# Down projection of a conditioned decoder block: 24 products of f-tile groups, or seven half-size products formed from sums

## The chip, the cores and the metric

The kernel runs on one core of a Trainium2 chip. The metric is device time in microseconds (us). The engines are PE (TensorE: matrix products; PEld is its weight load), DVE (VectorE), ACT (ScalarE), POOL (GpSimd) and SP (SyncE), the last of which issues most DMA transfers; ACT issues some. SBUF is the memory on the core with 128 partitions, PSUM holds the products' sums in banks of 128 x 512 fp32, DRAM lies outside the core.

## The reference

One block with S = 1024 tokens, D = 1024 channels and FF = 2816 hidden channels, all fp32. The part that the change touches is its last two lines.

```
h = rms_norm(x, norm_mix_g) * (1 + sc1) + sh1
proj = h @ w_in + b_in
y_conv  = silu(layer_norm(conv31(a))) @ w_conv_pw + b_conv_pw
y_mlstm = sigmoid(o_pre) * mlstm(q, k, v, gates)
x = x + g1 * ((g_conv * y_conv + g_mlstm * y_mlstm) @ w_out)
...
h = rms_norm(x, norm_ffn_g) * (1 + sc2) + sh2
gt, up = split(h @ w_ffn_up)
x = x + g2 * ((silu(gt) * up) @ w_ffn_down)
return rms_norm(x, final_norm_g)
```

## The kernel before

An fp32 product is made of three fp32r products: each operand is split into hi (a copy on ACT) and lo (raw minus hi, on DVE), and hi x hi, lo x hi and hi x lo are summed in PSUM. An instruction multiplies a stationary 128 x 128 block with a moving block of 128 x 512.

The program runs in stages: modulation and first norm, the input projection beside convolution and mLSTM, the output projection, the up projection with the SwiGLU, and the down projection with the final norm. The framework's scheduler decides the order of instructions on each engine, from the order in which the code gives them out and from its own timeline.

**Up projection.** FF is cut into 22 f-tiles of 128 channels; the loop at L1232 takes f = 2 to 21, and f-tiles 0 and 1 run before it in halves of the tokens (L1221 to L1230). For each, `up_run` (L1118) makes seven products of half size with the moving tiles Bh/Bl, Th/Tl and Dh/Dl, and sums them to the gate half cg and the up half cu, each [128, 512] for two token halves. The last lines, L1148 to L1155, apply Silu, multiply, and store cg to act_d in DRAM as [f within tile, f-tile, token], two transfers of 256 KB for an f-tile, in pieces of 1 KB, through ACT's queue (SP's for the last f-tile). In the last pass four rows of w_down are loaded and split for the first group.

**Down projection.** The 22 f-tiles are taken in `groups` of 4, 4, 6 and 8 (L1158). Within a group the loop runs over 8 token tiles t of 128: `act_split` (L1175) loads this group's activations of the token tile, transposed as they were stored, and splits them (stationary operand, tiles wraw, whi, wlo); then for both halves of the 1024 output columns come 3 products for each f-tile of the group (L1299 to L1301). The weights are `down_raw` (L1160: a 128 x 1024 row block of w_down, multiplied by the row g2) and `down_split` (L1165: hi and lo in tiles fa or, for the third group, fb). One row block of the next group is prepared for each token tile (PACE). A group's sums are added to the residual x1 on DVE (L1303); in the last group `finish` (L1262) adds, squares with a sum, multiplies by the final norm's gain, scales by the reciprocal root (a power on POOL, L104) and stores.

**Memory.** The tiles xa and xb (pool `big`) and wraw, whi, wlo (pool `wp`) live through both stages. Pool `fp`, opened after the up projection (L1246), takes the space that the up projection's own pools (`up`, and `tp` with Th and Tl) held, so what it holds waits for their last readers. All DMA issues of SP and ACT share a rotation of eight semaphores.

Of the kernel before, what the change touches and what calls it, by code (L numbers as in the profile page):

```python
# [33 lines left out]
PACE = 1  # L34
# [9 lines left out]
MC0 = 6152  # L44
MM0 = MC0 + 1024


@with_exitstack
def hybrid_block(ctx: ExitStack, tc: tile.TileContext, x, c, w_ada, b_ada, norm_mix_g, w_in, b_in,
# [903 lines left out]
    act_d = dram.tile([128, FT, S], F32, name="act_d")  # L953
# [164 lines left out]
    def up_run(f, w, half=None):  # L1118
# [29 lines left out]
        for i in range(2):  # L1148
            nc.scalar.activation(cg[i], cg[i], AF.Silu)
            nc.vector.tensor_mul(cg[i], cg[i], cu[i])  # L1150
            dst = act_d[:, f, :].rearrange("p (a b c) -> p b a c", a=2, b=2)
            if half is None:
                (nc.sync if f == FT - 1 else nc.scalar).dma_start(dst[:, i], cg[i].rearrange("p (a c) -> p a c", a=2))
            else:
                nc.scalar.dma_start(dst[:, i, half, :], cg[i])  # L1155
        yield

    groups = [4, 4, 6, 8]  # L1158

    def down_raw(f, raw, row):  # L1160
        nc.sync.dma_start(raw, wdn[f * 128:(f + 1) * 128, :])
        nc.vector.tensor_mul(raw, raw, row)
        return raw

    def down_split(gidx, i, raw):  # L1165
        if gidx == 2:
            hi, lo = (fp.tile([128, D], F32R, name=f"fb{j}", tag=f"fb{j}", bufs=6) for j in range(2))
        else:
            tag = "xa" if gidx == 0 or (gidx == 3 and i < 4) else "xb"
            hi, lo = (big.tile([128, D], F32R, name=f"fa{j}", tag=tag) for j in range(2))  # L1170
# [4 lines left out]
    def act_split(f0, nf, t):  # L1175
        raw, hi, lo = (wp.tile([128, KT, 128], dt, name=n, tag=n)[:, 0:nf, :]
                       for n, dt in (("wraw", F32), ("whi", F32R), ("wlo", F32R)))
        nc.sync.dma_start(raw, act_d[:, f0:f0 + nf, t * 128:(t + 1) * 128])
        nc.scalar.activation(hi, raw, AF.Copy)  # L1179
        nc.vector.tensor_sub(lo, raw, hi.bitcast(F32))  # L1180
        return hi, lo
# [50 lines left out]
    for f in range(2, FT):  # L1232
        w_f, w = w, up_split(up_sums(f + 1)) if f + 1 < FT else None
        if f == FT - 1:
            row = kx("g2row")
            mod_row(1, row)
            raws = [down_raw(i, (k4 if i < 2 else kx)("draw"), row) for i in range(4)]
        steps = up_run(f, w_f)
        next(steps)
        next(steps)  # L1240
        if f == FT - 1:
            wd = [down_split(0, i, raw) for i, raw in enumerate(raws)]
# [43 lines left out]
    for gidx, nf in enumerate(groups):  # L1286
# [4 lines left out]
        for t in range(8):  # L1291
# [3 lines left out]
            if gidx < 3:  # L1295
                p = ps_mm()
# [40 lines left out]
```

## Time and profile before

| | us |
|---|---|
| median of 3 runs | 1733.2 (1731.33 to 1735.08) |
| the profiled execution | 1735.88 |
| its span | 1734.1 |
| down projection, first to last product | 1482.1 to 1728.1 |
| up projection, one f-tile at steady pace | 19.5 |

The profile comes from one execution. A page gives busy times by engine; a view by windows gives them for stretches of the span; a view by groups puts together instructions of one line and shape (busy time, mean ns of one, and behind the second bar the idle time ahead of them with what ended it); the list of waits says for which instruction an engine waited, how long in total, how often and the longest; the timeline lists instructions with start and length.

### The profile page before, as it was taken

The numbers are of one execution on the slowest core, as the hardware profiler recorded it, in microseconds if no ns is written. First come the engines' busy times: TensorE is split into PE (matmuls) and PEld (weight loads), VectorE is DVE, ScalarE is ACT, GpSimd is POOL, SyncE is SP. The second block draws the span as 40 slices with busy tenths as digits, with TensorE's granted clock in tenths as the row PEclk, the third lists the DMA queues.
The fourth block names the chain that finished last, engine by engine and source line by source line (L and its number), as shares of the span: only waits on it lengthen the run. The fifth ranks groups of instructions, "written<-read, shape, count | busy, mean of one in ns | idle before, by whom it ended". The sixth has DMA issues, their size and how long they took to land. (4 is left out here: it accounts for less than half of the span.)

```text
span 1734.1 us, 20875 instructions
## 1 busy us (share of the span) xinstructions
PE 1692.9 (98%) x8360; PEld 1418.6 (82%) x8360; DVE 1249.7 (72%) x1681; ACT 611.7 (35%) x809; POOL 52.7 (3%) x113
## 2 busy tenths in 40 slices
PE   5999999999999999999999998999999999999998
PEld 4788889888988888888888778888888888778887
DVE  6989998997799669446798668766666665685243
ACT  7424335323433253223522386322222222232122
POOL 0000001000001000000000000000000000000000
PEclk9999999999999999999999999999999999999999
DMA  9221120221111112243694743322222222653121
GB/s 320 63 62 49 37 71 28 61 73 49 37 49 61 61 49 61 73 146 98 209 376 167 230 152 104 98 86 85 86 73 75 84 81 96 226 168 101 58 94 52
DMA packets 194711, 179.91 MB, mean 104 GB/s; under 512 B 7463, under 2 KB 166711, under 8 KB 194615
## 3 DMA queue, kind: packets, MB, share of 16 engines
q1 hardware_dynamic: 177367, 146.61, 27.4%
q10 hardware_dynamic: 17248, 31.99, 5.0%
q8 instruction: 65, 1.06, 0.3%
q14 instruction: 31, 0.25, 0.0%
HBM read 146.06 MB, written 32.51 MB: 103 GB/s over the span
## 5 line engine op out<-in xcount | busy, mean ns | idle before, releaser
L388 DVE SCALAR_TENSOR_TENSOR cacc<-a,col,cacc 128x1024 f32<-128x1024 f32 x240 | 306.8, 1286 | 3.9 <-ACT cacc L386 1.4
L158 PE MATMUL mm<-hh,wlo 128*128 128x512 f32 x864 | 271.2, 391 | 1.5 <-DVE wlo L149 1.5
L158 PE MATMUL mm<-hl,whi 128*128 128x512 f32 x864 | 272.5, 392 | 0.0
L158 PE MATMUL mm<-hh,whi 128*128 128x512 f32 x864 | 271.6, 392 | 0.0
L158 PEld LDWEIGHTS mm<-hh,wlo 128*128 128x128 f32 x864 | 160.3, 188 | 33.6 <-DVE wlo L149 2.7
L158 PEld LDWEIGHTS mm<-hl,whi 128*128 128x128 f32 x864 | 161.0, 188 | 32.1 <-issue 0.5
L158 PEld LDWEIGHTS mm<-hh,whi 128*128 128x128 f32 x864 | 160.5, 188 | 31.6
L148 ACT ACTIVATE whi<-wraw 128x1024 fp32r<-128x1024 f32 x61 | 64.7, 1061 | 226.5 <-PE mm L158 171.3
L149 DVE TENSOR_TENSOR wlo<-wraw,whi 128x1024 fp32r<-128x1024 f32 x61 | 74.5, 1222 | 28.7 <-ACT whi L148 25.2
L1114 PE MATMUL mm<-Bh,gh 128*128 128x512 f32 (+1 forms) x192 | 71.5, 375 | 2.9 <-ACT gh L1051 1.5
L1115 PE MATMUL mm<-Bl,gh 128*128 128x512 f32 (+1 forms) x192 | 71.5, 373 | 0.6 <-DVE Bl L1033 0.6
L604 PE MATMUL mm<-wlo,hh 128*128 128x256 f32 x256 | 72.0, 282 | 0.0
L1116 PE MATMUL mm<-Bh,gl 128*128 128x512 f32 (+1 forms) x192 | 71.2, 371 | 0.0
L1303 DVE TENSOR_TENSOR x<-x,mm 128x1024 f32<-128x1024 f32 x24 | 29.3, 1219 | 52.0 <-PE mm L1301 49.6
L1179 ACT ACTIVATE whi<-wraw 128x512 fp32r<-128x512 f32 (+2 forms) x32 | 25.3, 792 | 114.8 <-PE mm L1301 75.8
L535 DVE SCALAR_TENSOR_TENSOR cacc<-qkraw,col,cacc 128x1024 f32<-128x1024 f32 x48 | 61.5, 1282 | 4.9 <-ACT cacc L533 4.5
L603 PE MATMUL mm<-whi,hh 128*128 128x256 f32 x192 | 54.6, 284 | 0.0
L605 PE MATMUL mm<-whi,hl 128*128 128x256 f32 x192 | 54.2, 283 | 0.0
L1299 PE MATMUL mm<-fa,whi 128*128 128x512 f32 x128 | 50.6, 396 | 1.6 <-DVE cu L1142 0.9
L1300 PE MATMUL mm<-fa,wlo 128*128 128x512 f32 x128 | 50.5, 395 | 1.2 <-DVE wlo L1180 1.2
L1301 PE MATMUL mm<-fa,whi 128*128 128x512 f32 x128 | 50.6, 395 | 0.0
L1052 DVE TENSOR_TENSOR ul<-uraw,uh 128x1024 fp32r<-128x1024 f32 x20 | 24.5, 1225 | 35.4 <-ACT uh L1051 35.4
(444 smaller groups left out, 3893.1 us busy)
## 6 DMA issues: line engine op xcount, KB each, us to landing
wraw<-in_w_in_dram SPq DMA_DIRECT2D x64, 512.0 KB
awt<-in_w_ada_dram SPq DMA_DIRECT2D x32, 512.0 KB
graw<-in_w_ffn_up_dram SPq DMA_DIRECT2D x24, 512.0 KB
uraw<-in_w_ffn_up_dram SPq DMA_DIRECT2D x22, 512.0 KB
draw<-in_w_ffn_down_dram SPq DMA_DIRECT2D x22, 512.0 KB
act_d<-cg ACTq DMA_DIRECT2D x38, 256.0 KB
wad<-in_w_ada_dram SPq DMA_DIRECT2D x16, 512.0 KB
wraw<-in_w_out_dram SPq DMA_DIRECT2D x16, 512.0 KB
```

Source lines behind the costliest of these rows:

```text
L148: nc.scalar.activation(hi, raw, AF.Copy)
L149: (eng or nc.vector).tensor_sub(lo, raw, hi.bitcast(F32))
L158: nc.tensor.matmul(flat(acc)[:, a:b], lhs[:, k, :], rhs[k][:, a:b], start=(first and k == 0), stop=(last and k == kt - 1))
L388: nc.vector.scalar_tensor_tensor(acc, a[:, j:j + S], dw_col(j, ct), acc, op0=OP.mult, op1=OP.add)
L535: nc.vector.scalar_tensor_tensor(cv, raw[:, j:j + S], wcol(j), cv, op0=OP.mult, op1=OP.add)
L603: nc.tensor.matmul(o, hh[k][:, ts_], his[k], start=False, stop=False)
L604: nc.tensor.matmul(o[:, 0:256], hh[k][:, ts_], los[k], start=False, stop=False)
L605: nc.tensor.matmul(o, hl[k][:, ts_], his[k], start=False, stop=(k == KT - 1))
L1114: nc.tensor.matmul(o, a, rh, start=(k == 0), stop=False)
L1115: nc.tensor.matmul(o, a, rl, start=False, stop=False)
L1116: nc.tensor.matmul(o, b, rh, start=False, stop=(k == 3))
L1299: nc.tensor.matmul(o, hi[:, i, :], his[i][:, a:b], start=(i == 0), stop=False)
```

## The change

The down projection becomes seven products of half size in Winograd's form. The activations (as seen by the product) are cut into quadrants X11, X12, X21, X22 by tokens and by even and odd f-tiles, w_down into W11, W12, W21, W22 by even and odd f-tiles and by column halves. Of the activations seven combinations are needed: X11, X12, X22 and the sums XS1 = X21 + X22, XS2 = XS1 - X11, XS3 = X11 - X21, XS4 = X12 - XS2. They are made in `act_out`, at the end of each `up_run`, by one DVE operation on an even f-tile and three on an odd one, and each is stored to a DRAM tensor of its own, [128, 4 token tiles, 11, 128], through ACT's queue: seven transfers of 256 KB for two f-tiles, in pieces of 512 bytes. The weights' combinations are made in the down projection: `WSTEP` says for each product i which quadrant is loaded afresh (into `reg`), which second one (`other`), and the sign; `w_form` makes the difference in place and splits it; a product has six units u of two f-tiles each (the last of one). `TURN` says at which of the four steps of a product the units of the next product are formed, `WTAG` where their split tiles lie (xa, xb, wraw, whi, wlo).

The stage now has 28 steps n = (product i, token tile t). A step loads an X tile of 128 x 1408 two steps ahead, splits it one step ahead (`xr`, `xh`, `xl`, two buffers each), and does 33 products into one bank. `evict` takes the bank up: U and V, four tiles each, hold Winograd's partial sums. The factor g2 is no longer multiplied into the weights but into the results (`residual`, two DVE operations per half tile). The rows of tokens in the second half are finished in product 4, of the first half in products 5 and 6 (`last`). `x_first` loads and splits the first X tile, from the even f-tiles, within the up projection's last pass.

```
-PACE = 1
+X11, XS1, XS2, X22, XS3, XS4, X12 = range(7)
+W11, W12, W21, W22 = range(4)
+NU = 6
+UN = (2, 2, 2, 2, 2, 1)
+WSTEP = ((), (W12, W11, 1), (None, W22, -1), (None, W21, 1), (W22, W12, 1), (W22, None, 0), (W21, None, 0))
+WTAG = ((("xb", "xb"), ("xb", "xb"), ("xa", "xa"), ("xa", "xa"), ("xa", "xa"), ("xa",)),
+        (("xb", "xb"), ("xb", "xb"), ("xa", "wraw"), ("whi", "wlo"), ("wraw", "whi"), ("wlo",)))
+TURN = ((0, 1), (2, 3), (4, 5), ())
...
-    act_d = dram.tile([128, FT, S], F32, name="act_d")
+    FP = FT // 2
+    act_d = [dram.tile([128, 4, FP, 128], F32, name=f"act_d{i}") for i in range(7)]
+    pair = {}
...
-            dst = act_d[:, f, :].rearrange("p (a b c) -> p b a c", a=2, b=2)
-            if half is None:
-                (nc.sync if f == FT - 1 else nc.scalar).dma_start(dst[:, i], cg[i].rearrange("p (a c) -> p a c", a=2))
+        act_out(f, half, cg, cu)
+        yield
+    def act_out(f, half, cg, cu):
+        ts_ = slice(0, 4) if half is None else slice(2 * half, 2 * half + 2)
+        def out(i, t):
+            nc.scalar.dma_start(act_d[i][:, ts_, f // 2, :], t.rearrange("p (a c) -> p a c", c=128))
+        if f % 2 == 0:
+            out(X11, cg[0])
+            nc.vector.tensor_sub(cu[0], cg[0], cg[1])
+            out(XS3, cu[0])
+            pair[half] = cg, cu[1]
+            return
+        (x11, x21), s4 = pair[half]
+        out(X12, cg[0])
+        out(X22, cg[1])
+        nc.vector.tensor_add(x21, x21, cg[1])
+        out(XS1, x21)
+        nc.vector.tensor_sub(x11, x21, x11)
+        out(XS2, x11)
+        nc.vector.tensor_sub(s4, cg[0], x11)
+        out(XS4, s4)
+    wdq = wdn.rearrange("(j i p) e -> i p j e", i=2, p=128)
+    def w_load(t, quad, u):
+        nc.sync.dma_start(t, wdq[quad // 2][:, 2 * u:2 * u + UN[u], quad % 2 * 512:quad % 2 * 512 + 512])
+    def w_tiles(i, u):
+        got = []
+        for tag in WTAG[i % 2][u]:
+            if tag[0] == "x":
+                t = big.tile([128, 2, 512], F32R, name="wd", tag=tag)
             else:
+                t = wp.tile([128, 2, 512], F32R, name="wd", tag=tag)
+            got.append(t)
+        return (got[0][:, 0:1], got[0][:, 1:2]) if u == NU - 1 else got
+    def w_split(i, u, raw):
+        hi, lo = w_tiles(i, u)
         nc.scalar.activation(hi, raw, AF.Copy)
         nc.vector.tensor_sub(lo, raw, hi.bitcast(F32))
         return hi, lo
+    def x_first():
+        out = []
+        for a, b in ((0, KT), (KT, FP)):
+            raw, hi, lo = (wp.tile([128, KT, 128], dt, name=n, tag=n)[:, 0:b - a, :]
+                           for n, dt in (("wraw", F32), ("whi", F32R), ("wlo", F32R)))
+            nc.sync.dma_start(raw, act_d[X11][:, 0, a:b, :])
+            nc.scalar.activation(hi, raw, AF.Copy)
+            nc.vector.tensor_sub(lo, raw, hi.bitcast(F32))
+            out += [(hi[:, k, :], lo[:, k, :]) for k in range(b - a)]
+        return out
...
         if f == FT - 1:
-            row = kx("g2row")
-            mod_row(1, row)
-            raws = [down_raw(i, (k4 if i < 2 else kx)("draw"), row) for i in range(4)]
+            raws = [k4("draw") if u < 2 else kx("draw") for u in range(4)]
+            raws = [t.rearrange("p (j e) -> p j e", j=2) for t in raws]
+            for u in range(4):
+                w_load(raws[u], W11, u)
         steps = up_run(f, w_f)
         next(steps)
+        wd = []
+        if f == FT - 1:
+            tail = [k2("draw").rearrange("p (j e) -> p j e", j=1) for _ in range(3)]
+            for j, t in enumerate(tail):
+                nc.sync.dma_start(t, wdq[0][:, 8 + j:9 + j, 0:512])
+            wd = [w_split(0, u, raws[u]) for u in range(2)]
         next(steps)
         if f == FT - 1:
-            wd = [down_split(0, i, raw) for i, raw in enumerate(raws)]
+            xp = x_first()
+            wd += [w_split(0, u, raws[u]) for u in range(2, 4)]
+            hi, lo = w_tiles(0, 4)
+            for j in range(2):
+                nc.scalar.activation(hi[:, j:j + 1], tail[j], AF.Copy)
+                nc.vector.tensor_sub(lo[:, j:j + 1], tail[j], hi[:, j:j + 1].bitcast(F32))
+            wd += [(hi, lo), w_split(0, 5, tail[2])]
     ups.close()
...
+    x1 = [fp.tile([128, D], F32, name=f"x1_{t}") for t in range(8)]
+    ss = fp.tile([128, 8, 4], F32, name="ssf")
     grow, g2row = (fp.tile([128, D], F32, name=n) for n in ("grow", "g2row"))
+    reg = [fp.tile([128, UN[u], 512], F32, name=f"reg{u}") for u in range(NU)]
+    U = [fp.tile([128, 512], F32, name=f"U{t}") for t in range(4)]
+    V = [fp.tile([128, 512], F32, name=f"V{t}") for t in range(4)]
+    def tok(half, t):
+        return t // 2 * 4 + half * 2 + t % 2
+    other = {}
+    def w_fetch(i, u):
+        fresh, second, _ = WSTEP[i]
+        if fresh is not None:
+            w_load(reg[u], fresh, u)
+        if second is not None:
+            other[u] = fp.tile([128, 2, 512], F32, name="other", tag="other", bufs=3)[:, 0:UN[u]]
+            w_load(other[u], second, u)
+    def w_form(i, u):
+        sign = WSTEP[i][2]
+        if sign > 0:
+            nc.vector.tensor_sub(reg[u], reg[u], other[u])
+        elif sign < 0:
+            nc.vector.tensor_sub(reg[u], other[u], reg[u])
+        return w_split(i, u, reg[u])
+    def x_fetch(n):
+        raw = fp.tile([128, FP, 128], F32, name="xr", tag="xr", bufs=2)
+        nc.sync.dma_start(raw, act_d[n // 4][:, n % 4])
+        return raw
+    def x_split(raw):
+        hi, lo = (fp.tile([128, FP, 128], F32R, name=n, tag=n, bufs=2) for n in ("xh", "xl"))
+        nc.scalar.activation(hi, raw, AF.Copy)
+        nc.vector.tensor_sub(lo, raw, hi.bitcast(F32))
+        return [(hi[:, k, :], lo[:, k, :]) for k in range(FP)]
+    spares = []
+    def bank():
+        if not spares:
+            m = [ps_mm(), ps_mm()]
+            spares.extend([m[1][:, 1], m[1][:, 0], m[0][:, 1], m[0][:, 0], ps_c, ps_n, ps_a, ps_c])
+        t = spares.pop()
+        return t() if callable(t) else t
+    def down_mm(o, xp, wd, a, b):
+        for k in range(FP):
+            (xh, xl), (wh, wl) = xp[k], [t[:, k % 2, a:b] for t in wd[k // 2]]
+            nc.tensor.matmul(o, xh, wh, start=(k == 0), stop=False)
+            nc.tensor.matmul(o, xl, wh, start=False, stop=False)
+            nc.tensor.matmul(o, xh, wl, start=False, stop=(k == FP - 1))
+    def residual(t, cs, p):
+        nc.vector.tensor_mul(p, p, g2row[:, cs])
+        nc.vector.tensor_add(x1[t][:, cs], x1[t][:, cs], p)
+    def square(t, cs, p, i):
+        nc.scalar.activation(p, x1[t][:, cs], AF.Square, scale=1.0 / 32, accum_out=ss[:, t, i:i + 1])
+    def store(t):
+        rsqrt(ss[:, t, 3:4], ss[:, t, 2:3])
+        r = ss[:, t, 3:4]
+        rows = out2[t * 128:(t + 1) * 128, :]
+        for i, (a, b) in enumerate(HALVES):
+            if i:
+                nc.scalar.activation(x1[t][:, a:b], x1[t][:, a:b], AF.Copy, scale=r)
+            else:
+                nc.vector.tensor_scalar(x1[t][:, a:b], x1[t][:, a:b], r, None, op0=OP.mult)
+            nc.sync.dma_start(rows[:, a:b], x1[t][:, a:b])
+    LEFT, RIGHT = slice(0, 512), slice(512, 1024)
+    def evict(i, t, p):
+        if i == 0:
+            nc.scalar.activation(U[t], p, AF.Copy)
+            residual(tok(0, t), LEFT, p)
+        elif i == 1:
+            nc.scalar.activation(V[t], p, AF.Copy)
+        elif i == 2:
+            nc.vector.tensor_add(U[t], U[t], p)
+            nc.vector.tensor_add(V[t], V[t], U[t])
+        elif i == 3:
+            nc.vector.tensor_sub(U[t], U[t], p)
+        elif i == 4:
+            x = tok(1, t)
+            nc.vector.tensor_add(U[t], U[t], p)
+            nc.vector.tensor_add(p, V[t], p)
+            residual(x, RIGHT, p)
+            residual(x, LEFT, U[t])
+            square(x, RIGHT, p, 1)
+            square(x, LEFT, U[t], 0)
+            nc.vector.scalar_tensor_tensor(ss[:, x, 2:3], ss[:, x, 0:1], EPS, ss[:, x, 1:2], op0=OP.add, op1=OP.add)
+            nc.vector.tensor_mul(x1[x], x1[x], grow)
+            store(x)
+        elif i == 5:
+            x = tok(0, t)
+            nc.vector.tensor_add(p, V[t], p)
+            residual(x, RIGHT, p)
+            square(x, RIGHT, p, 1)
+            nc.vector.tensor_mul(x1[x][:, RIGHT], x1[x][:, RIGHT], grow[:, RIGHT])
...
+    N = 28
+    raw_x = {1: x_fetch(1)}
+    for u in TURN[0]:
+        w_fetch(1, u)
     mod_row(1, g2row)
+    nc.sync.dma_start(x1[tok(0, 0)], x1_d[tok(0, 0)])
+    ready, nxt = wd, []
+    for n in range(N):
+        i, t = divmod(n, 4)
+        if n + 2 < N:
+            raw_x[n + 2] = x_fetch(n + 2)
+        if n == 0:
             nc.sync.dma_start(grow, bass.AP(tensor=final_norm_g.tensor, offset=final_norm_g.offset, ap=[[0, 128], [1, D]]))
+        if n < 7:
+            x = tok((n + 1) // 4, (n + 1) % 4)
+            nc.sync.dma_start(x1[x], x1_d[x])
+        later = x_split(raw_x.pop(n + 1)) if n + 1 < N else None
+        if i < 6:
+            for u in TURN[t]:
+                nxt.append(w_form(i + 1, u))
+        for u in TURN[(t + 1) % 4]:
+            if i + 1 + (t == 3) < 7:
+                w_fetch(i + 1 + (t == 3), u)
+        if i < 6:
+            p = bank()
+            down_mm(p, xp, ready, 0, 512)
+            evict(i, t, p)
+        else:
+            last(t, xp, ready)
+        xp = later
+        if t == 3:
+            ready, nxt = nxt, []
```

How the order of instructions moves is seen at three places. The first is SP's queue where the up projection ends and the down projection begins. Names: `act_d` the stored activations, `x_..._d` the residual rows (x1), `draw` rows of w_down in the up projection's space, `mrow_d` the row g2. Before:

```order
L1153 DMA act_d<-cg 128x2x256 x2
L945 DMA g2row<-mrow_d_7547 128x1024
L1250 DMA x_0_11528<-x_d_7559 128x1024
L1161 DMA draw<-in_w_ffn_down_dram 128x1024
L1250 DMA x_1_11569<-x_d_7560 128x1024
L1161 DMA draw<-in_w_ffn_down_dram 128x1024
L1250 DMA x_2_11610<-x_d_7561 128x1024
L1250 DMA x_3_11651<-x_d_7562 128x1024
L1178 DMA wraw<-act_d 128x4x128
L1250 DMA x_4_11692<-x_d_7563 128x1024
```

After, from the rest of the first X tile (`wraw`) on; `xr` are the X tiles of steps 1 and 2:

```order
L1211 DMA wraw<-act_d_7567 128x384
L1324 DMA xr<-act_d_7567 128x1408
L1188 DMA reg_11640<-in_w_ffn_down_dram 128x2x512
L1188 DMA other<-in_w_ffn_down_dram 128x2x512
L1188 DMA reg_11641<-in_w_ffn_down_dram 128x2x512
L1188 DMA other<-in_w_ffn_down_dram 128x2x512
L952 DMA g2row<-mrow_d_7547 128x1024
L1423 DMA x_0_11629<-x_d_7559 128x1024
L1324 DMA xr<-act_d_7567 128x1408
L1430 DMA grow<-in_final_norm_g_dram 128x1024
L1433 DMA x_1_11630<-x_d_7560 128x1024
```

The last store of the up projection has moved to ACT's queue; its place at the head of SP's queue is taken by the X tile of step 1, and between the X tiles of steps 1 and 2 stand two units of both weight quadrants, g2 and a residual row. The queue goes on with two units' loads and x_4, and then, from the X tile of step 3 to that of step 4 and the last `other`:

```order
L1324 DMA xr<-act_d_7567 128x1408
L1188 DMA reg_11644<-in_w_ffn_down_dram 128x2x512
L1188 DMA other<-in_w_ffn_down_dram 128x2x512
L1188 DMA reg_11645<-in_w_ffn_down_dram 128x512
L1433 DMA x_5_11634<-x_d_7564 128x1024
L1433 DMA x_2_11631<-x_d_7561 128x1024
L1433 DMA x_3_11632<-x_d_7562 128x1024
L1433 DMA x_6_11635<-x_d_7565 128x1024
L1433 DMA x_7_11636<-x_d_7566 128x1024
L1188 DMA other<-in_w_ffn_down_dram 128x2x512
L1324 DMA xr<-act_d_7568 128x1408
L1188 DMA other<-in_w_ffn_down_dram 128x512
```

All but the last small unit of product 1's weights and five residual rows have come ahead of the first X tile of product 1.

The second place is ACT at the start of the down projection. Before, it only splits activations (`whi`) and weights (`fa`), and sums are not its work:

```order
L1179 ACTIVATE whi<-wraw 128x512 x2
L1171 ACTIVATE fa_11559<-draw 128x1024
L1171 ACTIVATE fa_11600<-draw 128x1024
L1179 ACTIVATE whi<-wraw 128x512 x3
L1171 ACTIVATE fa_11641<-draw 128x1024
L1171 ACTIVATE fa_11682<-draw 128x1024
```

After, with the copies `U` of the banks pc, pa and pn (steps 0 to 3), the copies `xh` of the X tiles and `wd` of the weights:

```order
L1371 ACTIVATE U_11646<-pc 128x512
L1329 ACTIVATE xh<-xr 128x1408
L1202 ACTIVATE wd<-reg_11640 128x1024
L1202 ACTIVATE wd<-reg_11641 128x1024
L1329 ACTIVATE xh<-xr 128x1408
L1371 ACTIVATE U_11647<-pa 128x512
L1202 ACTIVATE wd<-reg_11642 128x1024
L1371 ACTIVATE U_11648<-pn 128x512
L1329 ACTIVATE xh<-xr 128x1408
L1202 ACTIVATE wd<-reg_11643 128x1024
L1371 ACTIVATE U_11649<-pc 128x512
```

The copies of X tiles 1 and 3 (and 4) have come to stand behind the copy of the bank that the step just ahead of them fills.

The third place is DVE in product 5 of the down projection; V are partial sums, `mm` banks of steps 21 and 22, `xl` the lo part of an X tile. Before, in the last group, DVE has the sums of a token tile and then the split of the next tile but one:

```order
L1270 TENSOR_TENSOR x_2_11610<-x_2_11610,pa 128x512
L1272 TENSOR_TENSOR o<-x_2_11610,grow 128x512
L1270 TENSOR_TENSOR x_2_11610<-x_2_11610,pn 128x512
L1272 TENSOR_TENSOR o<-x_2_11610,grow 128x512
L1180 TENSOR_TENSOR wlo<-wraw,whi 128x1024
```

After:

```order
L1393 TENSOR_TENSOR mm<-V_11651,mm 128x512
L1350 TENSOR_TENSOR mm<-mm,g2row 128x512
L1393 TENSOR_TENSOR mm<-V_11652,mm 128x512
L1330 TENSOR_TENSOR xl<-xr,xh 128x1408
L1351 TENSOR_TENSOR x_1_11630<-x_1_11630,mm 128x512
L1350 TENSOR_TENSOR mm<-mm,g2row 128x512
```

The split of the X tile of step 23 has come to stand behind the first operation on the bank of step 22.

92 lines of the change are left out of this document (19 added, 73 removed).

## The prediction

> **What bounds the kernel now.** The page's first lines come first, then the busy time by stretches over the last stage, the pace of single products in the timeline, and PE's waits.
>
> ```profile
> span 1734.1 us, 20875 instructions
> PE 1692.9 (98%) x8360; PEld 1418.6 (82%) x8360; DVE 1249.7 (72%) x1681; ACT 611.7 (35%) x809; POOL 52.7 (3%) x113
> 1482.00:1728.00 246.00, 243.96 (x1080) 200.38 (x1080) 123.68 (x141) 58.19 (x87) 3.80 (x7) 0.99 0.36 120
> 1580.00:1636.00 56.00, 56.00 (x242) 44.88 (x241) 17.86 (x17) 7.22 (x8) 0.00 (x0) 1.00 0.16 48
> 1652.00:1720.00 68.00, 68.00 (x302) 56.31 (x301) 28.42 (x46) 19.90 (x39) 3.80 (x7) 1.00 0.23 78
> PE mm L1300 <- DVE wlo L1180: 1.2, 1, 1.2
> PE mm L1299 <- DVE cu L1142: 0.9, 1, 0.9
> PE mm L1299 <- DVE x L1303: 0.8, 1, 0.8
> ```
>
> The reader is to see that TensorE is the bound: 98% of the span, and 243.96 of 246.00 us in the down projection (columns: stretch, length, busy time of PE, PEld, DVE, ACT, POOL, granted clock, share of DMA, GB/s). DVE works half of it, DMA 0.36. PE's waits from 1440 us on add up to 2.9 us. So the time of the stage is a count of products times their pace, and the pace stands in the timeline (start, duration, engine, line):
>
> ```profile
> 1704.30 0.39 PE L1301 MATMUL pc<-fa,whi 128*128 128x512 f32 x1
> 1704.53 0.39 PE L1299 MATMUL pc<-fa,whi 128*128 128x512 f32 x1
> ...
> 1599.99 0.39 PE L1299 MATMUL mm<-fb,whi 128*128 128x512 f32 x1
> 1600.22 0.39 PE L1300 MATMUL mm<-fb,wlo 128*128 128x512 f32 x1
> ...
> 1727.36 0.28 PE L1300 MATMUL pa<-fa,wlo 128*128 128x256 f32 x1
> 1727.48 0.28 PE L1301 MATMUL pa<-fa,whi 128*128 128x256 f32 x1
> ...
> 1482.11 0.47 PE L1299 MATMUL mm<-fa,whi 128*128 128x512 f32 x1 [0.87 <-DVE cu L1142]
> ...
> 1728.15 0.42 DVE L1270 TENSOR_TENSOR x<-x,pa 128x256 f32<-128x256 f32 x1 [1.66 <-PE pa L1301]
> ```
>
> The 0.39 is the length of a pipelined product; what counts is start to start. Two groups differ: with a weight tile fa as moving operand about 0.227 us, with fb about 0.233. Over the two long stretches above, 68.00/302 and 56.00/242 (a few start before and end behind) agree; I take 0.2267 and 0.2333. The 256-wide ones take 0.12.
>
> **The change part by part.** *Products.* Before: 1080 instructions, of which 744 go at 0.2267 (168.7 us), 288 with fb (three groups of 96) at 0.2333 (67.2) and 48 of 256 columns at 0.1197 (5.7): 241.6. After: 7 products x 4 token tiles x 11 x 3 = 924, in 957 instructions, 891 of 512 columns and 66 of 256. Their weight tiles stand where fa and the wraw/whi/wlo tiles stood, in the two pools that this change leaves as they were, so I take fa's pace: 202.0 + 7.9 = 209.9. Difference **-31.7 us**.
>
> *Stalls of before.* From 1482.11 to the last product's end at about 1728.1 are 246.0 us, 4.4 more than 241.6, and 0.9 wait ahead of it. These 5.3 us belong to the old order: **-5.3**, and the new order's stalls are counted below.
>
> *The start.* This is the largest cost. Let T be the end of the up projection's last product. Then 24 of step 0's 33 products are left (9 are placed ahead of it): 24 x 0.2267 = 5.4 us; three more steps of 33 x 0.2267 = 7.48 make product 0 last until T+27.9 if nothing is late. SP's queue in the new order holds, at X tile 1 (`xr`), a tile that lies on the last up operands, so nothing behind it can be issued before T. Up to X tile 2 it has 4480 KB to move, to X tile 3 8256, to the fifth subtrahend (`other`) 12608, to X tile 4 (product 1's first) 13312.
>
> ```profile
> 1484.00:1488.00 4.00, 4.00 (x19) 3.31 (x18) 0.61 (x2) 0.10 (x1) 0.00 (x0) 1.00 0.75 223
> ...
> 1492.00:1496.00 4.00, 4.00 (x19) 3.27 (x18) 3.96 (x5) 1.70 (x2) 0.00 (x0) 1.00 1.03 421
> ...
> 1481.00:1509.00 28.00, 27.13 (x120) 22.23 (x119) 15.45 (x18) 5.18 (x7) 0.00 (x0) 1.00 0.85 309
> ...
> 856.00:916.00 60.00, 60.00 (x270) 48.41 (x269) 55.01 (x76) 10.02 (x14) 0.00 (x0) 1.00 1.06 379
> ```
>
> The DMA engines are full in before too at this place: 28 us at 309 GB/s, 421 in its best 4 us, and 379 over 60 us elsewhere in the program. I take 381 (the mean of the full windows from 1488 to 1508 is 382). Ahead come a run-up of 1.75 us (a quarter of 4 us empty in the first row, and two issues) and the five act stores of the last f-tile, 1280 KB: 3.4 us at that rate, 6.9 if their 512-byte pieces go at half of it; no such piece is in the trace of before, and I take 5. So X tile 2 lands at T + 6.75 + 4480 x 1.024/381 = T+18.8, tile 3 at T+28.9, tile 4 at T+42.5.
>
> A landed X tile has to be split before its step starts: an ACT copy and a DVE subtraction of 1408 columns.
>
> ```profile
> L1180 DVE TENSOR_TENSOR wlo<-wraw,whi 128x1024 fp32r<-128x1024 f32 x8 | 9.8, 1219 | 0.0
> L1180 DVE TENSOR_TENSOR wlo<-wraw,whi 128x768 fp32r<-128x768 f32 x8 | 7.6, 952 | 0.0
> L1179 ACT ACTIVATE whi<-wraw 128x1024 fp32r<-128x1024 f32 x8 | 8.5, 1065 | 38.9 <-issue 24.0 <-PE mm L1301 14.9
> L1179 ACT ACTIVATE whi<-wraw 128x768 fp32r<-128x768 f32 x8 | 6.8, 849 | 43.0 <-PE mm L1301 43.0
> L1179 ACT ACTIVATE whi<-wraw 128x512 fp32r<-128x512 f32 x16 | 10.0, 627 | 32.9 <-PE mm L1301 18.0 <-DMA wraw<-act_d 10.5 <-issue 2.6
> ```
>
> 256 columns more cost 267 ns on DVE and 216 on ACT, so 1408 take about 1.62 and 1.39 us. Besides, on ACT the copies of tiles 3 and 4 stand behind the copy U of the step just ended (0.6), which waits for that step's last product: even with its data there, such a step cannot start sooner than 0.6 + 1.4 + 1.6 = 3.6 us behind the one before. Step 1 starts at about T+9, step 2 near T+21.6, step 3 at T+32.6 (29.1 + 3.6), step 4 when tile 4 is split: T+42.5 + 3.0 and some 0.7 for the weight work that lies between on ACT and DVE, T+46.2. Against T+27.9 that is **+18.4**. Bounds: at 421 GB/s and 3.4 us of stores, tile 4 lands at T+37.5, +13.4; at 309 and 6.9 it lands at T+52.8, +28.7.
>
> *The clock.* Long waits of PE have a price behind them:
>
> ```profile
> 1542.25:1545.66 3.41, 1.48 (x6) 1.05 (x6) 3.03 (x4) 0.00 (x0) 0.00 (x0) 1.00 0.62 190
> 1545.66:1549.07 3.41, 3.41 (x9) 2.67 (x8) 3.27 (x4) 1.91 (x3) 0.00 (x0) 0.50 0.55 195
> ...
> 1047.29:1050.70 3.41, 2.10 (x18) 1.90 (x17) 1.28 (x3) 2.19 (x4) 0.00 (x0) 1.00 1.01 381
> ```
>
> A window with PE at 43% is followed by one at half the clock, in which 3.41 us do the work of 1.7; one with 62% is not. The starts of steps 2, 3 and 4 each have such a window. Two of the three I count on the path at 1.9 us each, **+3.8** (0 to 5.7): where the next X tile is late anyway, the slow step is hidden. The Trainium skill ("TensorE: Matmul & The Clock Gate", section "What's actually happening") has the clock halved after a window that was idle; by that rule only the longest gap (6 us) holds a full one, and the sum would be 1.9 lower. The 43% row speaks against so strict a reading, so I stay with it.
>
> *Late steps.* Where ACT or DVE stand in line, a step starts late though its data are there. On DVE, the split of tile 23 stands behind the eviction of step 22: its first half needs 0.7, the split 1.6, **+2.2** (0 to 2.3). Tiles 7 and 21 stand behind long work of the same kind, **+1.0** together (0 to 3.7). Changes of bank and product elsewhere cost what the list of waits shows for one such change, 0.8 to 1.2: **+1.2** (0 to 3).
>
> *Up projection.* Four DVE operations more for each pair of f-tiles.
>
> ```profile
> L1150 DVE TENSOR_TENSOR cg<-cg,cu 128x512 f32<-128x512 f32 x4 | 2.6, 686 | 0.0
> 1271.00:1290.50 19.50, 19.50 (x86) 15.79 (x85) 12.65 (x18) 5.58 (x7) 0.00 (x0) 1.00 0.27 83
> 1060.00:1080.00 20.00, 18.43 (x146) 17.23 (x146) 17.81 (x36) 14.57 (x24) 0.00 (x0) 1.00 0.13 40
> ```
>
> 4 x 0.69 = 2.7 us in 39, where DVE is busy 12.65 of 19.50 us: PE's own work hides it, and it would cost 11 x 2.7 = 30 us if it didn't. Where the halves of f-tiles 0 and 1 run (1060 to 1100), DVE is busy 17.81 of 20 and PE already waits. There 8 operations of 256 columns (0.42 each in the row at 1728.15) are 3.4 us: **+1.2** taken, 0 to 3.4. The stores are twice as many, at 83 GB/s and a share of 0.27: hidden. The g2row products that left the weights were beside PE's work too; nothing is gained there.
>
> *Tail.* PE's last product to the end is 1728.1 to 1734.1 before; one 256-wide product with g2row more on that path: **+0.4**.
>
> Sum: -31.7 - 5.3 + 18.4 + 3.8 + 2.2 + 1.0 + 1.2 + 1.2 + 0.4 = -8.8 us. The profiled execution took 1735.9 (span 1734.1 and 1.8 around it), so 1727.1; it lies 2.7 above the median of 1733.2, and on the median's footing that is 1724.4, said as **1725**.
>
> **The rivals.** *Cheap start.* Rates at 421 GB/s, stores at 3.4, late steps lost in the slack of a DVE that is about 75% busy: -37.0 + 13.4 + 1.9 + 0.4 and 1.0 of rest is -20.3, 1713. For it speaks the 421 row; against it the 60 us at 379.
>
> *DVE as the bound (slower).* Every split, weight difference and eviction goes through one DVE queue: 27 x 1.62 (44 us), six products of weight splits (41), four of weight differences (27), evictions and finishing (59): 171 us in some 235, against 123.68 in 246 now. In each product all weight units of the next must be through, and each step's X split stands behind the evictions. If a step starts late by 2.2 us at six places more (or by 2.2 and 1.9 of slow clock at three), 12 to 13 us are added: 1737. It turns slower than before from 12.3 us of further stalls. For it: the two rows of X splits already seen behind evictions; against: the X tiles are fetched two steps ahead and split one step ahead.
>
> *The pace isn't kept.* If the new weight tiles go as fb does, 891 x 0.0066 = 5.9 us come back: 1730, and the change of the pace was only that of fewer products. For it: two paces within one kernel; against: the tiles stand at fa's places.
>
> *Stores drawn out.* ACT's queue holds five stores of 512-byte pieces while SP's queue moves 2 to 5.6 KB pieces. If the engines take turns by piece, the stores finish only when SP's loads thin out; SP's issues that share their semaphores wait for them, a gap of about 3 us in the loads (the stores' time at 381 GB/s): 1728. The Trainium skill ("DMA: Bandwidth & Descriptors", section "Queues, rings and completion order") has each engine switch between queues packet by packet, which would do this. No row of before has such a mix.
>
> **How the numbers follow.** Forecast 0.43, cheap start 0.20, DVE as the bound 0.20, pace 0.09, drawn-out stores 0.08. A difference of 0.2% (3.5 us) is about what a measurement of this kernel can tell from no change, so faster means below 1729.7. The forecast's own bounds reach 1710 to 1736, and give faster in about 0.35 of its 0.43; with the cheap start, and most of the stores' case, 0.62. Slower is the DVE case and a rest: 0.20. The remainder, mostly the pace, is 0.18. The range takes in the cheap start and most of the DVE case: 1708 to 1739.
>
> **What would show it.** In the profile of the changed kernel: products at 0.2267 start to start in all seven products (0.2333 is the third rival); DMA full for about 40 us behind T, at 381 GB/s; PE's first products of steps 2, 3 and 4 near T+21, T+32 and T+46, released by DVE's split of `xr`, with windows at half clock behind; thereafter PE all but full, with a wait of about 2 us at step 23; some 6.4 us from the last product to the end. The prediction is wrong if product 1 starts before T+38 or after T+56, or if PE waits for DVE or ACT at many later steps by more than 5 us in all.

## The result and the profile after

| | before | after |
|---|---|---|
| median, us | 1732.5 (4 runs, 1731.3 to 1735.1) | 1743.7 (4 runs, 1742.6 to 1746.2) |
| span of the profiled execution, us | 1734.1 | 1741.6 |

The change makes the kernel slower by 0.6% (ratio 1.006, 95% interval 1.0048 to 1.0072), where 1725 had been predicted. Of the page of the changed kernel the first two lines, and of its view by stretches the rows that the prediction named (same columns as before):

```profile
span 1741.6 us, 20859 instructions
PE 1678.0 (96%) x8237; PEld 1401.4 (80%) x8237; DVE 1317.1 (76%) x1773; ACT 645.0 (37%) x835; POOL 56.9 (3%) x113
```

```profile
1483.00:1735.00 252.00, 227.32 (x950) 180.86 (x948) 165.78 (x190) 90.28 (x110) 8.04 (x7) 0.95 0.61 210
1560.00:1590.00 30.00, 30.00 (x131) 24.31 (x130) 21.90 (x23) 10.83 (x12) 0.00 (x0) 1.00 0.78 267
1510.85:1514.27 3.42, 2.00 (x9) 1.29 (x7) 0.72 (x2) 1.39 (x2) 0.00 (x0) 1.00 1.06 395
1514.27:1517.68 3.41, 1.66 (x6) 1.17 (x7) 3.33 (x3) 0.52 (x2) 0.00 (x0) 1.00 1.03 407
1517.68:1521.09 3.41, 3.41 (x10) 2.66 (x9) 1.23 (x1) 1.01 (x1) 0.00 (x0) 0.50 1.02 402
1271.00:1290.50 19.50, 19.50 (x86) 15.80 (x85) 13.34 (x19) 5.57 (x7) 0.00 (x0) 1.00 0.27 81
```

PE has less to do (15 us less in all), but now it waits: it is busy for 227 of 252 us in the down projection, at a mean clock of 0.95, where it was busy for 243.96 of 246 before. The timeline of PE in that stage, reduced to the ends and to the products ahead of which PE stood (in brackets the idle time and what ended it), shows where. T, the end of the up projection's last product, is taken where the product behind it starts, 1483.27.

```profile
1483.04 0.39 PE L1125 MATMUL mm<-Th,s3l 128*128 128x512 f32 x1
1483.27 0.39 PE L1345 MATMUL pc<-wd,whi 128*128 128x512 f32 x1
...
1492.93 0.49 PE L1345 MATMUL pa<-wd,xh 128*128 128x512 f32 x1 [4.02 <-ACT xh L1329]
1494.60 0.80 PE L1346 MATMUL pa<-wd,xl 128*128 128x512 f32 x1 [1.17 <-DVE xl L1330]
...
1514.80 0.50 PE L1345 MATMUL pc<-wd,xh 128*128 128x512 f32 x1 [1.95 <-ACT xh L1329]
...
1528.67 0.80 PE L1345 MATMUL mm<-wd,xh 128*128 128x512 f32 x1 [2.90 <-ACT xh L1329]
1531.19 0.79 PE L1346 MATMUL mm<-wd,xl 128*128 128x512 f32 x1 [1.72 <-DVE xl L1330]
1541.21 0.50 PE L1345 MATMUL mm<-wd,xh 128*128 128x512 f32 x1 [0.69 <-ACT V L1374]
1557.50 0.50 PE L1345 MATMUL mm<-wd,xh 128*128 128x512 f32 x1 [0.69 <-ACT V L1374]
1604.65 0.47 PE L1345 MATMUL mm<-wd,xh 128*128 128x512 f32 x1 [0.87 <-DVE U L1379]
1621.10 0.47 PE L1345 MATMUL mm<-wd,xh 128*128 128x512 f32 x1 [0.87 <-DVE U L1379]
1659.52 0.40 PE L1345 MATMUL mm<-wd,xh 128*128 128x512 f32 x1
...
1668.87 0.50 PE L1345 MATMUL mm<-wd,xh 128*128 128x512 f32 x1 [1.52 <-ACT xh L1329]
1671.28 0.80 PE L1346 MATMUL mm<-wd,xl 128*128 128x512 f32 x1 [1.91 <-DVE xl L1330]
1689.76 0.50 PE L1345 MATMUL pc<-wd,xh 128*128 128x512 f32 x1 [1.56 <-ACT xh L1329]
1693.39 0.79 PE L1346 MATMUL pc<-wd,xl 128*128 128x512 f32 x1 [3.13 <-DVE xl L1330]
...
1700.73 0.39 PE L1345 MATMUL mm<-wd,xh 128*128 128x512 f32 x1
...
1708.40 0.39 PE L1346 MATMUL pc<-wd,xl 128*128 128x512 f32 x1
...
1711.74 0.50 PE L1346 MATMUL pa<-wd,xl 128*128 128x512 f32 x1 [0.39 <-DVE xl L1330]
...
1719.29 0.40 PE L1345 MATMUL pn<-wd,xh 128*128 128x512 f32 x1
...
1734.65 0.28 PE L1347 MATMUL mm<-wd,xh 128*128 128x256 f32 x1
```

There are three groups. The start, up to the row at 1531.19 (steps 1, 3 and 4), was foreseen, but for the cause of step 1's wait. The four rows from 1541.21 to 1621.10 are steps 5, 7, 13 and 15; each waits for the operation that reads the bank of the step before it. And from 1659.52 (step 20) to 1719.29 (step 26) six steps take 59.8 us, where six at the stage's steady 7.67 us would take 46.0: 13.7 us are lost in product 5 and just behind it. By the program's operand names, PE doesn't take those steps in their order: what begins at 1668.87 is step 22, most of it, ahead of step 21, and what begins at 1689.76 is step 24, ahead of step 23. The rows show the second swap: PE fills pc (step 24) first, from 1700.73 on mm (step 23), and from 1708.40 on the rest of pc. The prediction took the steps to run in order. From step 5 on PE's waits add up to 11.6 us, where the prediction had named more than 5 as a sign against itself.

### The profile page after: what moved, and what is told of

Same layout as the page of the kernel before. It is cut to its first block, busy times and chain, and to the rows that moved or that the text cites. A ratio compares the mean times of both kernels' runs of the same rounds, so it can differ in the third digit from the quotient of the medians.

```text
span 1741.6 us, 20859 instructions
## 1 busy us (share of the span) xinstructions
PE 1678.0 (96%) x8237; PEld 1401.4 (80%) x8237; DVE 1317.1 (76%) x1773; ACT 645.0 (37%) x835; POOL 56.9 (3%) x113
## 5 line engine op out<-in xcount | busy, mean ns | idle before, releaser
L1329 ACT ACTIVATE xh<-xr 128x1408 fp32r<-128x1408 f32 x27 | 37.0, 1375 | 80.1 <-PE mm L1347 43.9
L1345 PE MATMUL mm<-wd,xh 128*128 128x512 f32 (+1 forms) x143 | 56.9, 399 | 7.5 <-ACT xh L1329 4.4
L1346 PE MATMUL mm<-wd,xl 128*128 128x512 f32 (+1 forms) x143 | 57.0, 398 | 3.6 <-DVE xl L1330 3.6
L1347 PE MATMUL mm<-wd,xh 128*128 128x512 f32 (+1 forms) x143 | 56.5, 395 | 0.0
L1330 DVE TENSOR_TENSOR xl<-xr,xh 128x1408 fp32r<-128x1408 f32 x27 | 43.8, 1621 | 9.3 <-ACT xh L1329 9.2
L611 PEld LDWEIGHTS mm<-wlo,hh 128*128 128x128 f32 x256 | 48.7, 190 | 0.0
```

The source lines that it names most:

```text
L611: nc.tensor.matmul(o[:, 0:256], hh[k][:, ts_], los[k], start=False, stop=False)
L1345: nc.tensor.matmul(o, xh, wh, start=(k == 0), stop=False)
L1346: nc.tensor.matmul(o, xl, wh, start=False, stop=False)
L1347: nc.tensor.matmul(o, xh, wl, start=False, stop=(k == FP - 1))
```

## The experiments

All are compared with the kernel before on the same chip. Ratios: e1 1.0074 (1.0059 to 1.0089), e2 1.0018 (1.0008 to 1.0028), e3 1.0038 (1.0025 to 1.0051), e5 0.9973 (0.9962 to 0.9984), e6 0.9926 (0.9909 to 0.9942), e7 0.9924 (0.991 to 0.9939), e8 0.9901 (0.9887 to 0.9916), e9 0.9858 (0.9841 to 0.9874), e10 0.9839 (0.9823 to 0.9855).

**e1_in_order: steps in order on PE.**

```
+            if k == 0 and ahead:
+                tc.add_manual_dep(first.ins, ahead[-1].ins.name, ORDER, reason="steps in order")
```

> The change, with one thing added: each step's first product is ordered behind the last product of the step before on PE. Theory S (the scheduler gave PE step 22 ahead of step 21 and step 24 ahead of step 23, so PE stands before an X tile that is not split while the step with a split tile stands behind it): PE's waits of 1.9, 2.4, 2.0, 3.6 and 0.8 us between 1667 and 1712 us of the changed kernel and the two half-clock stretches behind them go, 10 to 13 us in all; time 1731 to 1734. Rival D (DVE has more work than it can do in products 4 and 5): the waits move to the splits of X tiles 21 to 24 in their order and keep their sum within 3 us; time 1740 to 1744.

Measured: 1746.4 against 1734.5, as slow as the change or slower. Neither theory holds. PE's list of waits from 1655 to 1700 us of this run (engine, line waited for: total, times, longest):

```profile
PE mm L1348 <- ACT mm L1359: 12.1, 2, 7.6
```

The waits are no longer for X splits but for line 1359, the sum of squares on ACT, which ends the eviction: it takes a residual row and writes the squares into the bank of the step *before*. So step 21 cannot write its bank until the eviction of step 20 is through, though these are two banks. Both lie in one PSUM tile, [128, 2, 512]: `bank` hands out both halves of it one after the other. The scheduler had put step 22 ahead because step 21 was blocked, so the swapped order was the symptom, and the order that I forced made it wait in full. That reading is put to the test by e5.

**e2_rows_late: fewer bytes ahead of product 1.**

```
-        if n == 0:
-            nc.sync.dma_start(grow, ...)
-        if n < 7:
-            x = tok((n + 1) // 4, (n + 1) % 4)
-            nc.sync.dma_start(x1[x], x1_d[x])
+        if n == 8:
+            behind(nc.sync.dma_start(grow, ...))
+        if n < 3:
+            nc.sync.dma_start(x1[tok(0, n + 1)], x1_d[tok(0, n + 1)])
+        if 8 <= n < 12:
+            behind(nc.sync.dma_start(x1[tok(1, n % 4)], x1_d[tok(1, n % 4)]))
```

(`behind` orders the load on SP's queue behind the X tile just issued.)

> The change, with the final norm's gain and the four residual rows of the second token half (2560 KB) issued on SP behind X tile 10 instead of ahead of X tile 4. Theory L (the first steps wait for the bytes that stand ahead of their X tiles on SP's queue): 2560 x 1.024 / 381 = 6.9 us; the first product of step 4 comes at T+38.5 instead of T+45.4, steps 1 and 2 stay where they are; time 1735 to 1738. Rival A (the chain of ACT copies behind each step's bank, or the stores that go on, sets steps 3 and 4): step 4 moves by less than 2 us; time 1742 to 1745.

Measured: 1737.5 against 1734.5, 7 to 8 us better than the change: theory L by the time. By place it is both theories. T is 1483.82 in this run, and the timeline of PE has:

```profile
1493.56 0.49 PE L1351 MATMUL pa<-wd,xh 128*128 128x512 f32 x1 [4.10 <-ACT xh L1335]
...
1515.83 0.50 PE L1351 MATMUL pc<-wd,xh 128*128 128x512 f32 x1 [1.95 <-ACT xh L1335]
1517.56 0.50 PE L1352 MATMUL pc<-wd,xl 128*128 128x512 f32 x1 [1.23 <-DVE xl L1336]
...
1535.21 0.50 PE L1351 MATMUL mm<-wd,xh 128*128 128x512 f32 x1 [0.69 <-ACT V L1380]
```

The two rows at 1528.67 and 1531.19 of the change have no counterpart: step 4 waits for nothing. But it starts at T+42.8, not T+38.5, since step 3 still starts at T+32, behind the copy of step 2's bank. The loads had set step 4; with them out of the way the chain bank copy, X copy, X split of step 3 sets it. Step 5 comes 6.5 us sooner after T (T+51.4 instead of T+57.9), most of it because step 4 runs without its late split and without the slow clock. One thing changed beside the loads: on ACT the X copy of step 4 now stands ahead of the copy of step 3's bank (1520.77 and 1527.06), where the change has it behind (1527.26 and 1525.82). The run doesn't tell the two apart.

**e3_both: e1 and e2 together.**

> Both edits together. Theories S and L: the two gains add, as the places lie 130 us apart; time 1723 to 1728, faster than the kernel before by 0.3 to 0.5%. If DVE carries delays from the start to product 5, the sum falls short by more than 3 us.

Measured: 1740.3, 3 us worse than e2. It fell with theory S.

**e4_before_high: the place of an operand, in the kernel before.**

```
-        raw, hi, lo = (wp.tile([128, KT, 128], dt, name=n, tag=n)[:, 0:nf, :]
+        raw, hi, lo = (fp.tile([128, nf, 128], dt, name=n, tag=n, bufs=2) if f0 == 4 and n != "wraw" else
+                       wp.tile([128, KT, 128], dt, name=n, tag=n)[:, 0:nf, :]
```

> The kernel before, with the split activations (stationary operand) of its second group, 192 products, in tiles of the pool fp, at 144 KB of a partition and above, instead of below 95 KB; their weights (moving operand) stay below 70 KB. Theory H (a product takes 0.232 us start to start if either operand lies in the upper part of SBUF, 0.2267 if both lie in the lower): the 192 products go at 0.232 and the kernel is 1.0 us longer. Rival M (only the moving operand's place counts, as I had taken it): they stay at 0.2267.

Measured: 1734.6 in a single run beside 1734.5, no difference to be seen in the time. In the trace these products go at 0.229 start to start (the median over their group), the rest of their kind at 0.227. Rival M is out, since the stationary operand's place counts; theory H had the size wrong for this place.

**e5_banks: the double tiles taken alternately.**

```
-            spares.extend([m[1][:, 1], m[1][:, 0], m[0][:, 1], m[0][:, 0], ps_c, ps_n, ps_a, ps_c])
+            spares.extend([m[1][:, 1], m[0][:, 1], m[1][:, 0], m[0][:, 0], ps_c, ps_n, ps_a, ps_c])
```

> The change, with one list reordered: the four banks that lie in two double-bank PSUM tiles are taken as first half of tile 0, first half of tile 1, second half of tile 0, second half of tile 1, instead of both halves of tile 0 and then of tile 1. Theory B (a step that writes one half of a double tile is made to wait for the reader of the other half, so step 21 stands behind the eviction of step 20, and that is also why step 22 was put ahead of it): the waits before steps 5, 7, 13 and 15 go (0.85, 0.85, 1.04, 1.04), and so do the late steps 20 to 25 (some 13 us with the slow clock behind them): 15 to 17 us in all, 1727 to 1731 where the kernel before has 1733 to 1735. Rival D (DVE overloaded in products 4 and 5): waits for the X splits remain there, 1737 or more.

Measured: 1728.9 against 1733.5; by the ratios 0.9% below the change, 15 us. PE's list of waits from 1535 us on has one entry left:

```profile
PE mm L1345 <- ACT mm L1354: 2.1, 1, 2.1
```

It is again the second half of a double tile (step 22) that waits for the eviction of the first half (step 20), now two steps back. All else behind that time is gone, no X split is late there, and PE takes steps 20 to 25 in their order without being told to, with the same work on DVE (busy for 165.7 us from 1483 to 1720, 165.8 in the change from 1483 to 1735): theory B holds, and DVE is not the bound. DVE does set how long an eviction takes: in the changed kernel it is busy without a gap from 1654 to 1676, and the eviction of step 20, whose last product starts at 1666.95, ends only with its squares on ACT at 1674.8. What made PE feel this was the shared tile.

**e6_banks_late: e5 and e2 together.**

> The reordered banks, and the final norm's gain and the four residual rows of the second token half loaded behind X tile 10. Both theories (B and L): 7 to 8 us below the run with the banks alone, as the late rows gave 7 us to the change: 1719 to 1724. If the loads that were put off collide with products 2 and 3, less than 5 us.

Measured: 1720.7, 8 us below e5. The two effects add, as expected.

**e7_banks_late_low: split X tiles at 95 KB.**

```
+    low = [[fp.tile([128, FP, 128], F32R, name=f"{n}{i}") for n in ("xh", "xl")] for i in range(2)]
     x1 = [fp.tile([128, D], F32, name=f"x1_{t}") for t in range(8)]
...
-        hi, lo = (fp.tile([128, FP, 128], F32R, name=n, tag=n, bufs=2) for n in ("xh", "xl"))
+        hi, lo = low[n % 2]
```

> As the run before, with the split X tiles (stationary operand) allocated first in the pool fp, at 95 to 118 KB of a partition instead of 198 to 221 KB. Theory H (the pace of a product grows with the place of its operands: 0.227 below 95 KB, 0.229 with the stationary one at 144 KB, 0.232 at 200 KB): 0.227 to 0.229 start to start for the 858 products behind step 0, 3 to 4 us less. Rival: the place is not the cause (the pool, or the 1408-column tile): 0.232, no change.

Measured: 1720.4, no change in the time, but the pace did change. In the same 30 us PE now starts 134 products where the changed kernel had 131:

```profile
1560.00:1590.00 30.00, 30.00 (x134) 24.82 (x134) 24.70 (x26) 11.05 (x10) 0.00 (x0) 1.00 0.97 359
```

A step takes 7.48 us instead of 7.67. Most of what was won was lost at the start: step 1 comes at T+14.3 instead of T+9.6, step 4 at T+45.0 instead of T+42.3. So theory H holds for the pace, and the new place brought a wait of its own.

**e8_order: X12 x W21 as the second product.**

```
-WSTEP = ((), (W12, W11, 1), (None, W22, -1), (None, W21, 1), (W22, W12, 1), (W22, None, 0), (W21, None, 0))
+WSTEP = ((), (W21, None, 0), (W12, W11, 1), (None, W22, -1), (None, W21, 1), (W22, W12, 1), (W22, None, 0))
+XSTEP = (X11, X12, XS1, XS2, X22, XS3, XS4)
```

(with `evict` and `last` rearranged to match, and weights, g2, gain and rows ordered behind X tiles)

> As the run before, with the product X12 x W21 taken from the last place to the second (its weights need no difference: 2816 KB instead of 5632 KB ahead of step 4) and all other loads of the start ordered behind the X tiles of product 1. Theory L: X tile 4 stands behind 5632 KB, lands near T+22, and step 4 starts when PE has done product 0, T+33 to T+36 instead of T+43 (step 1 still waits for ACT until about T+10): 7 to 10 us less, 1706 to 1712. Rival: DVE has too much in the new product 1, which evicts and forms the next weights at once (about 9 us of work for a 7.6 us step), and the steps of products 1 and 2 come late: 1716 or more.

Measured: 1715.9 against 1733.5, 4 us below e7 instead of 7 to 10. Step 4 starts at T+41.3 instead of T+45.0; steps 2 to 4 wait for nothing any more, and no step of products 1 and 2 comes late, so DVE's work in the new product 1 costs nothing. The rival had the time nearly right, 1716 or more, but its mechanism is out. The run makes two changes at once, the order of the products and that of the loads, and doesn't tell them apart. Step 1 still starts at T+14.6. The timeline of ACT of this run:

```profile
1490.77 0.60 ACT L1381 ACTIVATE U<-pc 128x512 f32<-128x512 f32 x1 [8.26 <-DMA act_d<-cg]
1496.40 1.38 ACT L1339 ACTIVATE xh<-xr 128x1408 fp32r<-128x1408 f32 x1 [5.03 <-DMA reg<-in_w_ffn_down_dram]
```

ACT stands 5 us ahead of the X copy. The releaser named is a load that the copy doesn't need; the tile it writes, at 106 KB, lies on the last activations, whose stores have to land first. The next run tested that.

**e9_place: the X tile of step 1 elsewhere.**

```
-    low = [[fp.tile([128, FP, 128], F32R, name=f"{n}{i}") for n in ("xh", "xl")] for i in range(2)]
-    x1 = [fp.tile([128, D], F32, name=f"x1_{t}") for t in range(8)]
+    low = [[fp.tile([128, FP, 128], F32R, name=f"{n}0") for n in ("xh", "xl")]]
+    x1 = [fp.tile([128, D], F32, name=f"x1_{t}") for t in range(4)]
+    V = [fp.tile([128, 512], F32, name=f"V{t}") for t in range(4)]
+    low.append([fp.tile([128, FP, 128], F32R, name=f"{n}1") for n in ("xh", "xl")])
+    x1 += [fp.tile([128, D], F32, name=f"x1_{t}") for t in range(4, 8)]
```

> As the run e8_order, with the split X tile of step 1 at 131 KB of a partition instead of 106 KB (residual rows and partial sums lie between). In e8_order it lay where the last f-tile's activations wait to be stored, and step 1 came 14.6 us after the up projection's last product; theory P (its ACT copy waits until those stores have landed): without that wait ACT reaches the copy behind its store issues and the bank's copy, step 1 at T+9 to T+10 as in the change itself, 4 to 5 us less: 1710 to 1713. Rival: X tile 1 itself lands late in the new load order; no change.

Measured: 1710.2 against 1734.3, step 1 at T+9.3. In ACT's timeline the X copy now follows the bank's copy at once:

```profile
1492.35 0.60 ACT L1383 ACTIVATE U<-pc 128x512 f32<-128x512 f32 x1 [8.20 <-DMA act_d<-cg]
1492.84 1.37 ACT L1341 ACTIVATE xh<-xr 128x1408 fp32r<-128x1408 f32 x1
```

**e10_place_dve: that copy on DVE.**

```
+        if n == 1:
+            nc.vector.tensor_copy(hi, raw)
+        else:
+            nc.scalar.activation(hi, raw, AF.Copy)
```

> As e9_place, with the hi part of the X tile of step 1 copied by DVE instead of ACT. Theory Q (ACT issues five stores from T+3 to T+8, then copies the bank of step 0, and only then the X tile, while DVE is free): step 1 starts at about T+7.5 instead of T+9.5 and one stretch of slow clock is shorter: 2 to 3 us less than e9_place. Rival: X tile 1 has not landed by then; no change.

Measured: 1707.5 against 1734.3 (1703.7 to 1709.1), step 1 at T+6.5, 3 us less than e9. By the ratios it beats the kernel before by 1.6% and the change by 2.2%. PE's timeline and DVE's at that place:

```profile
1488.34 0.89 DVE L1342 CAST xh<-xr 128x1408 fp32r<-128x1408 f32 x1
1489.26 1.62 DVE L1345 TENSOR_TENSOR xl<-xr,xh 128x1408 fp32r<-128x1408 f32 x1
...
1489.28 0.50 PE L1360 MATMUL pa<-wd,xh 128*128 128x512 f32 x1 [0.81 <-DVE xh L1342]
1490.94 0.50 PE L1361 MATMUL pa<-wd,xl 128*128 128x512 f32 x1 [1.16 <-DVE xl L1345]
```

PE's gap is 2 us instead of 5, and the slow clock behind it does not come: in this run no stretch of half clock lies between T and the last products.

## Why the prediction was wrong

Term by term, on the profiled executions (1741.6 - 1734.1 = +7.5 us, where -8.8 had been forecast):

| term | forecast | measured | from |
|---|---|---|---|
| products and pace | -31.7 | -27.3 | 23 steps behind the start at 7.67 instead of 7.48 |
| stalls of before | -5.3 | -5.3 | not there any more |
| start, up to step 4 | +18.4 | +17.5 | step 4 at 1528.67, T+45.4 |
| clock, with step 4's late split | +3.8 | +4.0 | step 4 takes 12.54 us, 0.85 of it ahead of step 5 |
| late steps and changes of bank | +4.4 | +17.5 | 3.8 for steps 5, 7, 13, 15 (0.85 or 1.04 each, start to start); 13.7 from step 20 to 25 |
| up projection | +1.2 | 0 | T moved by 2.0, the 9 products put ahead of it; T differs by 2.7 between e7 and e9, which have the same up projection |
| tail | +0.4 | +0.7 | last product starts at 1734.65 |
| sum | -8.8 | +7.1 | +7.5 by the spans |

- **The step that failed is "Late steps"** and, in the same place, the 1.2 us for changes of bank: 4.4 together, 17.5 measured, 13 of the 16 us by which the forecast missed. I had priced what DVE's queue puts ahead of an X split. What decided was a wait that the program makes between two banks of one PSUM tile: e1 laid it bare (12.1 us in two waits for the other half's eviction), and e5 took 15 us away by a reordered list. The rival "DVE as the bound" had foreseen the sign and nearly the price (12 to 13 us); its mechanism was wrong, as e5 has the same DVE work and one wait of 2.1 us in place of 11.6. The prediction's reading of X tile 23 "behind the eviction of step 22" was a sign of the same thing: the scheduler had steps 22 and 24 ahead of 21 and 23, and I read the rows as if the steps were in order.
- **The pace**: 4.4 us of the third rival's 5.9 came true. The weight tiles do stand where fa stood; what had moved was the other operand. The split X tiles lie at 198 KB and above, where wraw, whi and wlo were below 95 KB, and e7 got 0.227 back by placing them low.
- **The start** was right in size, 17.5 against 18.4, and in most of its mechanism. DMA is full there (395 to 407 GB/s in the rows above, 381 taken), X tile 2 lands at T+18.8 as forecast, as the row of its copy on ACT below shows, and step 3 stands behind the copy of step 2's bank. With its loads put off in e2, step 4 comes 2.6 us sooner, and in e10 it starts at T+31.0. One part was not in my working: step 1 waited for ACT, which first issues five stores (e10), and came at T+9.7 for that reason and not for the load. It then ran in part at half clock, so step 2 found its tile split and waited for nothing; that it began at T+21.6 all the same, to the tenth as forecast, is luck.

```profile
1502.04 1.38 ACT L1329 ACTIVATE xh<-xr 128x1408 fp32r<-128x1408 f32 x1 [1.79 <-DMA xr<-act_d]
```

- **The clock** behaved as the rows of before had it: a stretch with PE at 1.66 of 3.41 us was followed by one at half clock, one with 2.00 of 3.42 was not. The Trainium skill ("TensorE: Matmul & The Clock Gate", section "What's actually happening") asks for an idle window; this trace doesn't agree, 49% busy was enough. The term itself agrees by luck: half clock came behind the starts of steps 1, 3 and 4, not 2, 3 and 4, and of the 4.0 us in the table 2.3 are the wait for step 4's lo part and 1.7 the clock. Start and clock together are 21.5 us measured, 22.2 forecast.
- **The stores** were not drawn out. SP's next issue stood behind them from 1484.8 to 1491.5, as the fourth rival has it (the first row below, from SP's list of waits from 1480 to 1530 us), and its queue ran out of loads. From 1490.2 to 1493.0 the engines moved 1942 packets of ACT's queue and 3 of SP's, at 346 GB/s (the other rows, from the DMA view of that stretch). So the loads had a gap of 3 us, and the stores filled it. From first to last packet they took 4.4 us, where the forecast's sum has 5 for them: the gap cost nothing more.

```profile
SPq L1188 <- DMA act_d<-cg: 7.0, 2, 6.7
q10 hardware_dynamic: 1942, 0.96, 114.6%
q1 hardware_dynamic: 3, 0.00, 0.4%
```

- **The up projection** hid its four operations, as far as can be seen: DVE went from 12.65 to 13.34 us of 19.50 in the stretch at 1271, and PE stayed full. Whether the 1.2 us in the halves of f-tiles 0 and 1 came is not shown, since T differs by more than that from run to run (1482.23 in e7, 1484.92 in e9).

## What to carry to other kernels

Count the products last: a form that saves an eighth of them pays only if every new wait is found, and the wait that decided here came from two banks handed out of one tile, which no engine's load shows. When a scheduler has put a step ahead of its turn, ask what blocks the step it passed; forcing the order back makes the block visible, removing the block makes the order right. Where buffers move to another pool, look at both operands' places, and at who still holds the memory under a tile that is needed first.

## What the runs showed of the hardware

- The pace of a 512-column product depends on where its operands lie in SBUF (the place is the one that the program allocates, the pace is read from the timeline). With the moving one below 95 KB of a partition it is 0.227 us with the stationary one below 118 KB (e7) and also at 131 to 142 KB (e9, every second step), 0.229 at 144 to 153 KB (e4) and 0.232 at 198 KB and above (the change). With the moving one at 144 KB and above it is 0.233 (the third group before). The cause was not looked for.
- At half clock, a stretch in which PE was 76% busy was not followed by full clock (the rows below, of the changed kernel), while at full clock a stretch with 58% was.

```profile
1493.78:1497.19 3.41, 2.59 (x6) 2.12 (x7) 2.29 (x3) 1.06 (x1) 0.00 (x0) 0.50 1.04 379
1497.19:1500.61 3.42, 3.42 (x9) 2.66 (x9) 2.94 (x4) 1.06 (x1) 0.00 (x0) 0.50 1.02 400
```

- Stores in pieces of 512 bytes went at 346 GB/s with nearly nothing beside them, loads in pieces of 2 KB and more at 395 to 407 (the changed kernel).
- A copy of 128 x 1408 from fp32 to fp32r took 0.89 us on DVE (e10) and 1.37 on ACT (e9).
